# More of an MLP's up projection by seven products of halves, and its down product made in one piece of five parts

## The chip, the cores and the metric

One Trainium2 chip, one of its cores. The metric is the device time of one execution in microseconds (us); lower is better. Kernel before: median 923.41 us of 3 runs (923.1 to 926.32).

## What is computed

A decoder trunk of one layer on 512 tokens of width 1024, all in float32: three token mixers with an output projection, then a gated MLP with a causal depthwise convolution, then a last norm. The change lies in the MLP:

```python
h2 = rms_norm(x, norm_ffn[l])                                        # 512 x 1024
up = causal_dwconv(h2 @ w_up[l], ffn_conv_w[l], ffn_conv_b[l])       # 512 x 6144
gate_h, val_h = jnp.split(up, 2, axis=-1)
x = x + (jax.nn.gelu(gate_h, approximate=True) * val_h) @ w_down[l]  # w_down 3072 x 1024
...
return rms_norm(x, final_norm)
```

## The kernel before

**Products.** Each float32 operand is split into a high and a low fp32r part (`split`, L95: ScalarE (ACT) writes the high part, L97, VectorE (DVE) the rest, L98), and each product is three TensorE (PE) matmuls, high by high, high by low and low by high (`mm3`, L100 to L104).

**Units.** The program is a list of units of PE work. Each has preparations, (lead, function) pairs, and `emit` (L183) writes a preparation out that many units ahead of its unit. The engines' queues keep very nearly the order in which this is written; each engine works through its queue in order.

**Up projection.** The 6144 channels are 24 pairs of a gate tile and a value tile of 128 channels. A *plain* pair is two units (`up_units`, L1187), each 24 matmuls of 512 columns and one 512 KB weight load, split two units ahead (`AHEAD`). A *fast* pair (`up_fast`, L1240) is made by seven products of halves (Winograd's form of Strassen's scheme): the pair's weights are four blocks B11 to B22 of 128 x 512, the tokens and the inner dimension are halved, and there are seven units a1, a2, c1, c2, b1, b2, b3, each 12 matmuls of 256 columns. Block sums are made by DMA: `load` (SP's queue) brings one block, and `add` (L1255, POOL's queue) adds another to it in SBUF. So B11 is split for a1, gets B12 added, is split for c1, gets B22 added, is split for b1, gets B21 added, is split for b3. DVE and ACT put the seven results together from PSUM (L1273 to L1278). Then `up_evac` (L1167: one ACT and two DVE instructions per tile, the convolution) and `up_mix` (L1182: gelu on ACT, product on DVE at L1184) give the activations of that tile.

In time, fast pairs overlap: one beat of eight units is b1 of the pair before, a1, a plain unit, b2 of the pair before, c1, a2, b3 of the pair before, c2.

**Down product.** Activations of tiles 0 to 19 (five *parts* of four tiles) are multiplied with `w_down` by seven products as well (`seven`, L285, with `down_fast`, L1297). Here a key (a1, a2, c1, c2, b1, b2, b3) has one unit per part, 12 matmuls of 512 columns in two PSUM banks, and after the last part the banks are read into the residual `x2` (`read`, L1337: one DVE instruction of 512 columns per bank and target, L1335). The preparations of an a1 unit are `sums` (L1301: six DVE instructions of 256 columns on the activations of its four tiles, three units ahead) and `act_ready` (L1324, the split of the sums, one unit ahead); of all, the weights' split two units ahead. Before, this is two calls, of three parts and of two; the second adds its a1 banks to what the first kept (`kept`, L1343). `blend` (L353) mixes plain units in: the 21 units of the first call among 14 plain ones (tiles 13 to 19), the 14 of the second among 8 (tiles 20 to 23, whose product goes by `halves`, L1402, to a last plain down product).

**Memory.** Tiles of 128 x 512 live in 51 slots (`NSLOT`); split weights of 1024 columns in four buffers for the high and four for the low parts (`NWB`, tags `whi`, `wlo`), so that the split of a weight waits for the end of the unit that used the buffer four weights earlier; whole 512 KB loads in three (`NRAW`).

Of the kernel before, what the change touches and what calls it, by code (L numbers as in the profile page):

```python
# [34 lines left out]
NF = FF // P  # L35
# [22 lines left out]
def trunk(ctx: ExitStack, tc: tile.TileContext, x, xT, mem, memT, par, wdecay, wch, wv, wg, wmk,  # L58
# [285 lines left out]
    def run(*parts):  # L344

        for p in parts:
            if isinstance(p, tuple):
                unit(*p)
            else:
                for v in p:  # L350
                    made_unit(*v) if isinstance(v, tuple) else step(v)

    def blend(us, fast, steps=()):  # L353

        for i, u in enumerate(us):
            unit(*u)
            for l, f in ((fast, lambda v: made_unit(*v)), (steps, step)):
                for v in l[len(l) * i // len(us):len(l) * (i + 1) // len(us)]:
                    f(v)
# [407 lines left out]
    b2 = [u for d in range(KD) for u in branch(2, oc, d)]  # L767
# [472 lines left out]
    def up_fast(i, keep):  # L1240

        src = lambda q: wup[NF * (int(q[2]) - 1) + i][:, HB * (int(q[1]) - 1):HB * int(q[1])]
        raw, w, st = {}, {}, {}

        def load(q):
            raw[q] = fslot()
            loads.append(nc.sync.dma_start(raw[q], src(q)))

        def ready(key, q, more=None):
            w[key] = rslot(), rslot()  # L1250
            split(*w[key], raw[q])
            if more:
                add(q, more)

        def add(q, more):  # L1255
            nc.gpsimd.dma_start(raw[q], src(more), accum_op=ALU.add)

        def run(key):
            if key == "a1":
                st["x"], st["o"] = bank((P, HT)), (fslot(), fslot())  # L1260
            elif key in ("a2", "c1"):
                st[key] = sbank((P, HT))
            ps = st["c1" if key[0] == "c" else "a2" if key == "a2" else "x"]
            hi, lo = w.pop(key)
            k = range(KD // 2)
            mm3(ps, [(*(a[:, j * P:(j + 1) * P] for a in (hi, lo)), *h2_part(key, j)) for j in k],
                key in ("a1", "a2", "c1"), True, key not in ("a1", "a2", "c1"))
            (g, v), tt = st["o"], nc.vector.tensor_tensor

            one, two = slice(0, HT), slice(HT, S)  # L1270
            if key in ("a1", "c1", "c2", "b3"):
                o = {"a1": g[:, one], "c1": v[:, two], "c2": v[:, one], "b3": g[:, two]}[key]
                nc.scalar.activation(o, ps, AF.Copy)  # L1273
            elif key == "a2":
                tt(out=g[:, one], in0=g[:, one], in1=ps, op=ALU.add)
            else:
                o = v[:, one if key == "b1" else two]
                tt(out=o, in0=o, in1=ps, op=ALU.subtract)  # L1278
            if key == "b3":
                up_mix(*(up_evac(a, NF * half + i) for half, a in enumerate((g, v))), i, keep)  # L1280

        pre = {
            "a1": [(8, lambda: load("B11")), (3, lambda: ready("a1", "B11", "B12"))],
            "a2": [(6, lambda: load("B21")), (3, lambda: ready("a2", "B21"))],
            "c1": [(2, lambda: ready("c1", "B11", "B22"))],
            "c2": [(6, lambda: load("B22")), (3, lambda: ready("c2", "B22"))],
            "b1": [(2, lambda: ready("b1", "B11", "B21"))],
            "b2": [(9, lambda: load("B12")), (6, lambda: add("B12", "B22")), (3, lambda: ready("b2", "B12"))],
            "b3": [(2, lambda: ready("b3", "B11"))],
        }  # L1290
        return {key: (p, lambda key=key: run(key)) for key, p in pre.items()}
# [105 lines left out]
    acts = {}  # L1397
# [4 lines left out]
    def halves(i, a):  # L1402
        acts[i] = rslot(), rslot()
        split(*acts[i], a)

    group = lambda first: lambda k: acts[first + k]
    us = up_units((0, 1, 2, 5, 8, 11), whole, 3)
    run(*us[:3], [lambda: h2_sums(0)], us[3], [lambda: h2_sums(1)], us[4], [lambda: h2_ready("c1", 0), lambda: h2_ready("c1", 1)],
        us[5], [lambda: h2_ready("c2", 0), lambda: h2_ready("c2", 1)])

    ahead = None
    for i, u in zip((3, 4, 6, 7, 9, 10), us[6:]):
        f = up_fast(i, whole)
        run([ahead["b1"]] if ahead else [], [f["a1"]], u)
        run([ahead["b2"]] if ahead else [], [f["c1"], f["a2"]], [ahead["b3"]] if ahead else [], [f["c2"]])
        if not ahead:
            run([lambda k=k, p=p: h2_ready(k, p) for k in ("b1", "b2") for p in range(2)])
        ahead = f
    us = up_units(range(12, 20), whole)
    run([ahead["b1"]], us[0], [ahead["b2"]], us[1], [ahead["b3"]])  # L1420
    blend(us[2:], down_fast(0, 3, group(0), True, False))
    blend(up_units(range(20, NF), halves), down_fast(3, 2, group(12), False, True))
    step(lambda: gain_rows(gfin))
    weave(down_units(wdown2, group(20), final, None, final_left, 2), [])

    emit()

# [90 lines left out]
```

## Time and profile before

| | |
|---|---|
| median of 3 runs | 923.41 us |
| profiled execution: time, span | 924.37 us, 922.6 us |
| PE busy | 912.0 us (99% of the span), 4606 matmuls |
| DVE busy | 657.2 us (71%) |
| ACT busy | 524.1 us (57%) |
| POOL busy | 128.1 us (14%) |
| granted PE clock, mean | 0.997 |

A row of the time line gives the start, the length, engine, line, operation and tiles, with `xN` for N merged instructions and in brackets the idle time before it and what ended it. Instructions of one engine overlap a little at their ends, so the step from start to start is what one costs in a queue without gaps, not its length. About 540 us into the span the up projection begins; the first down call stands at about 684 to 815 us, the second at 815 to 896 us.

### The profile page before, as it was taken

How to read it: one execution, taken by the hardware profiler on the slowest of the kernel's cores; microseconds unless marked ns; L12 is line 12 of the kernel's file. 1: busy time of each engine (PE TensorE's matmuls, PEld its weight loads, DVE VectorE, ACT ScalarE, POOL GpSimd, SP SyncE). 2: the span in 40 equal slices, each digit the busy share in tenths (PEclk: the TensorE clock that was granted, in tenths of full speed). 3: DMA queues.
4: the chain of work that ended last, by engine and by line, in shares of the span. 5: the costliest groups of instructions: out<-in, count | busy, mean ns of one | idle time of the engine just before them, and what ended most of it. 6: DMA issues, size and time to landing. Idle time of an engine off the chain costs nothing.

```text
span 922.6 us, 12732 instructions
## 1 busy us (share of the span) xinstructions
PE 912.0 (99%) x4606; PEld 784.1 (85%) x4606; DVE 657.2 (71%) x1168; ACT 524.1 (57%) x888; POOL 128.1 (14%) x168
## 2 busy tenths in 40 slices
PE   9999999999999999999999999999999999999997
PEld 7899888888889998888888898998988888888885
DVE  6997755665689568746766678767787757598765
ACT  7765655685865468474534446555555445445544
POOL 0010000000243430320000000222111130013102
PEclk9999999999999999999999999999999999999998
DMA  7446223213467884321157313675646785357622
GB/s 238 148 137 214 92 88 101 88 42 119 110 170 167 187 204 126 115 86 53 52 157 258 116 59 90 157 185 130 148 114 165 145 228 125 114 137 181 139 69 91
DMA packets 51183, 123.27 MB, mean 134 GB/s; under 512 B 6145, under 2 KB 14001, under 8 KB 51121
## 3 DMA queue, kind: packets, MB, share of 16 engines
q1 hardware_dynamic: 35648, 94.99, 31.6%
q0 software_dynamic: 15328, 27.21, 17.3%
q8 instruction: 36, 0.59, 0.3%
q10 hardware_dynamic: 144, 0.26, 0.1%
q14 instruction: 27, 0.21, 0.1%
HBM read 117.99 MB, written 3.67 MB: 132 GB/s over the span
## 4 chain that ended last, share of the span: by engine, by line
PE 87%; DMA 5%; DVE 3%; issue 2%; ACT 2%; POOL 0%; SPq 0%; DVEq 0%; POOLq 0%; ACTq 0%
PE mm L104 78%; DMA f<-in_wup 4%; PE sm L104 3%; DMA f<-in_wv 2%; PE mm L436 2%; DVE wlo L98 1%; DVE r L98 1%; ACT r L97 1%; PE sm L211 0%; PE sm L996 0%; PE sm L983 0%; PE sm L1010 0%; DVE f L810 0%; PE sm L1147 0%; PE sm L601 0%
## 5 line engine op out<-in xcount | busy, mean ns | idle before, releaser
L97 ACT ACTIVATE whi<-raw 128x1024 fp32r<-128x1024 f32 (+3 forms) x142 | 135.5, 961 | 144.4 <-PE mm L104 113.1
L98 DVE TENSOR_TENSOR wlo<-raw,whi 128x1024 fp32r<-128x1024 f32 (+3 forms) x142 | 157.4, 1113 | 82.8 <-ACT whi L97 39.4
L104 PE MATMUL mm<-whi,r 128*128 128x512 f32 (+2 forms) x568 | 171.2, 372 | 0.0
L104 PEld LDWEIGHTS mm<-whi,r 128*128 128x128 f32 x568 | 105.5, 188 | 15.9 <-ACT r L97 0.3
L104 PE MATMUL mm<-hh,whi 128*128 128x512 f32 x288 | 113.4, 394 | 0.0
L104 PE MATMUL mm<-hl,whi 128*128 128x512 f32 x288 | 112.8, 392 | 0.0
L104 PE MATMUL mm<-wlo,r 128*128 128x512 f32 (+2 forms) x284 | 105.7, 372 | 0.5 <-DVE wlo L98 0.5
L104 PE MATMUL mm<-h2l,whi 128*128 128x512 f32 x264 | 102.8, 390 | 0.0
L104 PE MATMUL mm<-h2h,whi 128*128 128x512 f32 x264 | 102.7, 390 | 0.0
L98 DVE TENSOR_TENSOR r<-f,r 128x512 fp32r<-128x512 f32 (+3 forms) x144 | 79.7, 577 | 23.0 <-ACT r L97 22.7
L104 PE MATMUL mm<-r,whi 128*128 128x512 f32 (+1 forms) x432 | 94.2, 367 | 0.0
L97 ACT ACTIVATE r<-f 128x512 fp32r<-128x512 f32 (+3 forms) x144 | 70.1, 535 | 34.1 <-DMA f<-in_wup 29.2
L98 DVE TENSOR_TENSOR wlo<-f,whi 128x512 fp32r<-128x512 f32 (+2 forms) x90 | 53.8, 631 | 47.5 <-ACT whi L97 40.6
L104 PEld LDWEIGHTS mm<-r,whi 128*128 128x128 f32 x432 | 75.2, 189 | 13.1
L97 ACT ACTIVATE whi<-f 128x512 fp32r<-128x512 f32 (+2 forms) x90 | 48.2, 579 | 62.5 <-PE mm L104 48.8
L104 PE MATMUL mm<-hh,wlo 128*128 128x512 f32 x288 | 71.4, 390 | 0.0
L104 PE MATMUL mm<-r,r 128*128 128x512 f32 (+2 forms) x336 | 65.7, 346 | 0.3 <-ACT r L97 0.3
L104 PE MATMUL mm<-h2h,wlo 128*128 128x512 f32 x264 | 65.2, 389 | 0.0
L104 PEld LDWEIGHTS mm<-hh,wlo 128*128 128x128 f32 x288 | 54.0, 188 | 11.2
L104 PEld LDWEIGHTS mm<-hh,whi 128*128 128x128 f32 x288 | 54.1, 188 | 10.8
L104 PEld LDWEIGHTS mm<-hl,whi 128*128 128x128 f32 x288 | 54.1, 188 | 10.7
L104 PEld LDWEIGHTS mm<-r,r 128*128 128x128 f32 (+1 forms) x336 | 53.3, 186 | 9.6 <-ACT r L97 0.5
(261 smaller groups left out, 1545.2 us busy)
## 6 DMA issues: line engine op xcount, KB each, us to landing
raw<-in_wch SPq DMA_DIRECT2D x39, 512.0 KB, 3.3
raw<-in_wup SPq DMA_DIRECT2D x36, 512.0 KB, 4.0
f<-in_wdown POOLq DMA_DIRECT2D x40, 256.0 KB, 7.0
raw<-in_wbr SPq DMA_DIRECT2D x24, 384.0 KB, 3.1
raw<-in_wdown SPq DMA_DIRECT2D x14, 512.0 KB, 3.8
f<-in_wup SPq DMA_DIRECT2D x24, 256.0 KB, 6.9
f<-in_wup POOLq DMA_DIRECT2D x24, 256.0 KB, 6.4
f<-in_wdown SPq DMA_DIRECT2D x20, 256.0 KB, 4.7
```

What stands on the lines that cost most here:

```text
L97: nc.scalar.activation(hi, src, AF.Copy)
L98: return (eng or nc.vector).tensor_tensor(out=lo, in0=src, in1=hi.bitcast(F32), op=ALU.subtract)
L104: nc.tensor.matmul(ps, lhsT=l, rhs=r, start=first and i == 0, stop=last and i == len(seq) - 1, skip_group_check=more)
L436: nc.tensor.matmul(ps[u], lhsT=w(a, u, k), rhs=xs["r"][k][j], start=k == 0 and i < n, stop=k == KD - 1 and i >= len(seq) - n)
```

## The change

Tiles 12, 13, 15, 16 and 18 become fast pairs too (eleven in place of six), each in a beat with a plain unit of tiles 5, 8, 11, 14, 17, 19. The down product is one call of five parts, its 35 units blended with the seven plain units that are left (the second of tile 20, then tiles 21, 22, 23): one plain unit, then five units of one key. Some leads change.

```diff
         pre = {
-            "a1": [(8, lambda: load("B11")), (3, lambda: ready("a1", "B11", "B12"))],
-            "a2": [(6, lambda: load("B21")), (3, lambda: ready("a2", "B21"))],
-            "c1": [(2, lambda: ready("c1", "B11", "B22"))],
+            "a1": [(10, lambda: load("B11")), (5, lambda: ready("a1", "B11", "B12"))],
+            "a2": [(7, lambda: load("B21")), (3, lambda: ready("a2", "B21"))],
+            "c1": [(3, lambda: ready("c1", "B11", "B22"))],
             "c2": [(6, lambda: load("B22")), (3, lambda: ready("c2", "B22"))],
             "b1": [(2, lambda: ready("b1", "B11", "B21"))],
-            "b2": [(9, lambda: load("B12")), (6, lambda: add("B12", "B22")), (3, lambda: ready("b2", "B12"))],
+            "b2": [(10, lambda: load("B12")), (7, lambda: add("B12", "B22")), (1, lambda: ready("b2", "B12"))],
             "b3": [(2, lambda: ready("b3", "B11"))],
         }
...
-    group = lambda first: lambda k: acts[first + k]
-    us = up_units((0, 1, 2, 5, 8, 11), whole, 3)
+    us = up_units((0, 1, 2), whole, 3)
...
+    us = up_units((5, 8, 11, 14, 17, 19), whole) + up_units(range(20, NF), halves)
     ahead = None
-    for i, u in zip((3, 4, 6, 7, 9, 10), us[6:]):
+    for i in (3, 4, 6, 7, 9, 10, 12, 13, 15, 16, 18):
         f = up_fast(i, whole)
-        run([ahead["b1"]] if ahead else [], [f["a1"]], u)
+        run([ahead["b1"]] if ahead else [], [f["a1"]], us.pop(0))
...
-    us = up_units(range(12, 20), whole)
-    run([ahead["b1"]], us[0], [ahead["b2"]], us[1], [ahead["b3"]])
-    blend(us[2:], down_fast(0, 3, group(0), True, False))
-    blend(up_units(range(20, NF), halves), down_fast(3, 2, group(12), False, True))
+    run([ahead["b1"]], us.pop(0), [ahead["b2"]], us.pop(0), [ahead["b3"]])
+    blend(us, down_fast(0, 5, lambda k: acts[k], True, True))
     step(lambda: gain_rows(gfin))
-    weave(down_units(wdown2, group(20), final, None, final_left, 2), [])
+    weave(down_units(wdown2, lambda k: acts[20 + k], final, None, final_left, 2), [])
```

How the queues stand at the start of the down product, at three places. *a1_0, a1_1, ...* are the a1 units of parts 0, 1, ...

**First place: DVE, where the weights of the first a1 units are split.** Before, the rows that begin with the split of a1_1's weights (`wlo_1312`). `f_1297` is the value half of plain tile 12, `f_1300` and `f_1301` the halves of fast tile 10, `f_1284` the gate half of tile 12.

```order
L98 TENSOR_TENSOR wlo_1312_6716<-f_1287_6571,whi_1311_6715 128x512
L98 TENSOR_TENSOR wlo_1312_6716<-f_1288_6572,whi_1311_6715 128x512
L1171 SCALAR_TENSOR_TENSOR f_1297_6631<-mm_1296_6606,prm_76,f_1297_6631 128x511
L1171 SCALAR_TENSOR_TENSOR f_1297_6631<-mm_1296_6606,prm_76,f_1297_6631 128x510
L1171 SCALAR_TENSOR_TENSOR f_1300_6656<-f_1255_6359,prm_76,f_1300_6656 128x511
L1184 TENSOR_TENSOR f_1284_6563<-f_1284_6563,f_1297_6631 128x512
L1171 SCALAR_TENSOR_TENSOR f_1300_6656<-f_1255_6359,prm_76,f_1300_6656 128x510
```

Of the change, the rows that begin with the split of a1_2's weights (`wlo_1471`). `f_1449` is the gate half of plain tile 20, `f_1456` and `f_1457` are the halves of fast tile 18; L1311 to L1313 are `sums`.

```order
L98 TENSOR_TENSOR wlo_1471_7653<-f_1439_7486,whi_1470_7652 128x512
L1311 TENSOR_TENSOR f_1452_7556<-f_1185_5944,f_1113_5533 128x256
L1171 SCALAR_TENSOR_TENSOR f_1449_7546<-mm_1448_7521,prm_76,f_1449_7546 128x511
L1312 TENSOR_TENSOR f_1453_7557<-f_1452_7556,f_1185_5944 128x256
L1171 SCALAR_TENSOR_TENSOR f_1449_7546<-mm_1448_7521,prm_76,f_1449_7546 128x510
L1313 TENSOR_TENSOR f_1185_5944<-f_1185_5944 128x256
L1311 TENSOR_TENSOR f_1452_7556<-f_1215_6127,f_1245_6308 128x256
L1171 SCALAR_TENSOR_TENSOR f_1456_7581<-f_1405_7271,prm_76,f_1456_7581 128x511
```

At both places the first row waits for its buffer, so for the end of the plain unit just ahead of the last pair's b3. Of the change it is followed at once by the sums of part 1, with the evacuations of tiles 18 and 20 between them.

**Second place: DVE, up to the split of a1_1's activation sums.** Before, `r_1318` (the low part of a1_1's sums) stands 24 rows behind `wlo_1312`, and the sums that precede it are those of parts 1 and 2.

```order
L1171 SCALAR_TENSOR_TENSOR f_1310_6711<-mm_1309_6686,prm_76,f_1310_6711 128x510
L1312 TENSOR_TENSOR f_1314_6722<-f_1313_6721,f_1173_5865 128x256
L1313 TENSOR_TENSOR f_1173_5865<-f_1173_5865 128x256
L1311 TENSOR_TENSOR f_1313_6721<-f_1300_6656,f_1233_6229 128x256
L98 TENSOR_TENSOR r_1318_6744<-f_1184_5942,r_1317_6743 128x256
```

Of the change, `f_1465` is the value half of plain tile 20, `r_1467` the low part of tile 20's activations (needed by the last down product only), `r_1469` the low part of a1_1's sums, 30 rows behind `wlo_1471`.

```order
L1171 SCALAR_TENSOR_TENSOR f_1465_7636<-mm_1464_7611,prm_76,f_1465_7636 128x511
L98 TENSOR_TENSOR wlo_1471_7653<-f_1440_7487,whi_1470_7652 128x512
L1171 SCALAR_TENSOR_TENSOR f_1465_7636<-mm_1464_7611,prm_76,f_1465_7636 128x510
L98 TENSOR_TENSOR wlo_1479_7687<-f_1446_7517,whi_1478_7686 128x512
L1184 TENSOR_TENSOR f_1449_7546<-f_1449_7546,f_1465_7636 128x512
L98 TENSOR_TENSOR wlo_1479_7687<-f_1447_7518,whi_1478_7686 128x512
L98 TENSOR_TENSOR wlo_1485_7719<-f_1454_7564,whi_1484_7718 128x512
L98 TENSOR_TENSOR r_1467_7643<-f_1449_7546,r_1466_7642 128x512
L98 TENSOR_TENSOR r_1469_7647<-f_1185_5944,r_1468_7646 128x256
```

The product of tile 20 (L1184), its split, and the weights of a1_2, a1_3 and a1_4 now stand ahead of a1_1's sums.

**Third place: ACT, the high part of a1_1's sums.** Before (`r_1317`), behind tile 13's gate half and a plain unit's weights:

```order
L1169 ACTIVATE f_1310_6711<-mm_1309_6686,prm_76 128x512
L97 ACTIVATE whi_1326_6794<-raw_1325_6792 128x1024
L97 ACTIVATE r_1317_6743<-f_1184_5942 128x256
L97 ACTIVATE r_1317_6743<-f_1214_6125 128x256
L1183 ACTIVATE f_1310_6711<-f_1310_6711 128x512
```

Of the change (`r_1468`), behind the weights of a1_4 (`whi_1484`, whose buffer is free when a1_0 ends) and the high part of tile 20's activations (`r_1466`, which waits for DVE's L1184 of `f_1449`):

```order
L1169 ACTIVATE f_1465_7636<-mm_1464_7611,prm_76 128x512
L97 ACTIVATE whi_1484_7718<-f_1454_7564 128x512
L97 ACTIVATE whi_1484_7718<-f_1455_7565 128x512
L97 ACTIVATE r_1466_7642<-f_1449_7546 128x512
L97 ACTIVATE r_1468_7646<-f_1185_5944 128x256
L97 ACTIVATE r_1468_7646<-f_1215_6127 128x256
```

PE's a1_1 unit begins with `r_1468`. On PE, before, a plain unit stands between a1_0 and a1_1; of the change a1_1 follows a1_0 at once.

## Rows read from the trace of the kernel before

**Rows 1.** The profile page: span, and the busy time of PE and DVE.
```profile
span 922.6 us, 12732 instructions
PE 912.0 (99%) x4606; PEld 784.1 (85%) x4606; DVE 657.2 (71%) x1168; ACT 524.1 (57%) x888; POOL 128.1 (14%) x168
```

**Rows 2.** Who waited for whom, PE's rows over the whole span: total us, times, longest. The two longest.
```profile
PE sm L211 <- DVE warm L207: 1.1, 1, 1.1
PE mm L104 <- DVE f L1278: 0.7, 1, 0.7
```

**Rows 3.** Time line of PE in a beat of fast pairs: one unit of a fast pair (601.02 to 602.46), then one plain unit (602.46 to 607.93).
```profile
601.02 0.28 PE L104 MATMUL mm<-h2h,r 128*128 128x256 f32 x1
...
602.46 0.40 PE L104 MATMUL mm<-h2h,whi 128*128 128x512 f32 x1
...
606.11 1.98 PE L104 MATMUL mm<-h2h,wlo 128*128 128x512 f32 x8
607.93 1.60 PE L104 MATMUL mm<-r,r 128*128 128x256 f32 x12
```

**Rows 4.** Time line of PE at the start of the down product: a1_0 (684.17 to 686.89), a plain unit, and two more down units (692.33 to 697.80).
```profile
684.17 0.39 PE L104 MATMUL mm<-whi,r 128*128 128x512 f32 x1
...
686.89 0.39 PE L104 MATMUL mm<-h2h,whi 128*128 128x512 f32 x1
...
692.33 0.39 PE L104 MATMUL mm<-whi,r 128*128 128x512 f32 x1
...
697.80 0.39 PE L104 MATMUL mm<-h2h,whi 128*128 128x512 f32 x1
```

**Rows 5.** Busy time by stage: stretch, its length, then us busy (and instructions) of PE, weight loads, DVE, ACT, POOL, the granted clock, the share of the DMA engines, GB/s. Three beats of fast pairs; the first down call; the second.
```profile
602.00:649.00 47.00, 46.28 (x315) 42.63 (x314) 32.58 (x53) 26.21 (x48) 9.07 (x11) 1.00 0.67 158
682.00:815.00 133.00, 133.00 (x589) 110.04 (x588) 95.43 (x161) 67.14 (x110) 19.35 (x22) 1.00 0.57 140
815.00:896.00 81.00, 81.00 (x358) 66.92 (x357) 66.46 (x110) 42.06 (x70) 12.32 (x14) 1.00 0.56 144
```

**Rows 6.** Time line of DVE at the start of the first down call.
```profile
677.53 1.29 DVE L98 TENSOR_TENSOR wlo<-f,whi 128x512 fp32r<-128x512 f32 x2 [0.80 <-PE mm L104]
...
680.85 0.69 DVE L1184 TENSOR_TENSOR f<-f,f 128x512 f32<-128x512 f32 x1
681.45 1.41 DVE L1171 SCALAR_TENSOR_TENSOR f<-f,prm,f 128x510 f32<-128x510 f32 x2
...
684.71 0.76 DVE L1311 TENSOR_TENSOR f<-f,f 128x256 f32<-128x256 f32 x2
685.38 0.42 DVE L1312 TENSOR_TENSOR f<-f,f 128x256 f32<-128x256 f32 x1
...
687.71 0.74 DVE L1171 SCALAR_TENSOR_TENSOR f<-mm,prm,f 128x510 f32<-128x510 f32 x1
688.37 0.42 DVE L1312 TENSOR_TENSOR f<-f,f 128x256 f32<-128x256 f32 x1
...
691.92 2.35 DVE L98 TENSOR_TENSOR wlo<-raw,whi 128x1024 fp32r<-128x1024 f32 x2
694.19 0.74 DVE L1171 SCALAR_TENSOR_TENSOR f<-mm,prm,f 128x511 f32<-128x511 f32 x1
```

**Rows 7.** Time line of ACT at the same place.
```profile
676.67 1.25 ACT L97 ACTIVATE whi<-f 128x512 fp32r<-128x512 f32 x2 [2.16 <-DMA f<-in_wdown]
677.83 0.76 ACT L1169 ACTIVATE f<-mm,prm 128x512 f32<-128x512 f32 x1
...
688.06 0.70 ACT L97 ACTIVATE r<-f 128x256 fp32r<-128x256 f32 x2
688.67 0.62 ACT L1183 ACTIVATE f<-f 128x512 f32<-128x512 f32 x1
```

**Rows 8.** The chain that ended last, in order of time, around PE's one wait of the up projection: start, us, what.
```profile
615.43 8.77 DMA f<-in_wup
624.20 0.02 issue
...
628.24 0.34 DVE f L1278
628.58 0.14 issue
628.72 1.91 PE mm L104 x12
```

**Rows 9.** Busy time by half microseconds at the end of the span, columns as in rows 5. PE's last matmul ends at 915.66 us.
```profile
915.50:916.00 0.50, 0.16 (x1) 0.00 (x0) 0.30 (x1) 0.50 (x1) 0.00 (x0) 1.00 0.82 307
...
917.00:917.50 0.50, 0.00 (x0) 0.00 (x0) 0.26 (x2) 0.44 (x3) 0.00 (x0) 1.00 0.85 319
917.50:918.00 0.50, 0.00 (x0) 0.00 (x0) 0.43 (x3) 0.00 (x0) 0.00 (x0) 0.83 0.69 246
918.00:918.50 0.50, 0.00 (x0) 0.00 (x0) 0.46 (x2) 0.29 (x1) 0.00 (x0) 0.50 1.03 389
```

**Rows 10.** DMA issues: queue, count, KB each, median us from issue to landing.
```profile
f<-in_wdown POOLq DMA_DIRECT2D x40, 256.0 KB, 7.0
f<-in_wup SPq DMA_DIRECT2D x24, 256.0 KB, 6.9
f<-in_wup POOLq DMA_DIRECT2D x24, 256.0 KB, 6.4
f<-in_wdown SPq DMA_DIRECT2D x20, 256.0 KB, 4.7
```

## The prediction

> **What bounds the kernel now.** I read the profile page first. PE is busy for 912.0 of 922.6 us, DVE for 657.2 [rows 1]. Then the waits: the longest that PE spends on another engine are 1.1 us at the very start and 0.7 us once in the up projection [rows 2]. So PE's queue is the time: whatever leaves it shortens the run, unless a gap opens. The third view, busy time by stage, shows where a gap could open. In the beats of fast pairs DVE works 32.6 of 47 us and ACT 26.2; in the first down call DVE works 95.4 of 133; in the second, with fewer plain units beside the down units, 66.5 of 81, which is 82% [rows 5]. PE waits in neither down call, but DVE is the engine that is nearest to it.
>
> All sums are made against the profiled execution, 924.37 us, which is 0.96 us above the median of the runs; I carry the difference over to the median, 923.4. A change below 0.5% (4.6 us, so 918.8 to 928.0) cannot be told from none.
>
> **The change part by part.**
>
> *PE's work.* A unit of a fast pair takes 602.46 - 601.02 = 1.44 us and a plain unit 607.93 - 602.46 = 5.47 us, from start to start [rows 3]. A plain pair is 2 x 5.47 = 10.94 us, a fast one 7 x 1.44 = 10.08: 0.86 us less. Five pairs change: **-4.3 us**. The saving is small because seven products of half the columns cost almost what two full units do. The down product keeps its 35 units of 2.73 us (two of them take 697.80 - 692.33 = 5.47 us [rows 4]): 0.
>
> *Five more beats.* A beat lasts 7 x 1.44 + 5.47 = 15.5 us and loads the other engines as the present ones do (DVE 69%, ACT 56%, DMA 158 GB/s [rows 5]). All work that comes with it (seven splits, eight 256 KB transfers in place of two of 512 KB per pair, the combining on DVE) is hidden there now, so 0. Without that cover one late accumulation per beat would cost what the one wait costs today, 0.7 us [rows 2].
>
> *The leads.* That one wait hangs on an accumulation that took 8.77 us to land [rows 8]: ACT and DVE stood behind it, and a subtraction that PE needed came late. The new leads give the split of B11 for a1 two units more and that for c1 one, so each accumulation on that chain starts earlier against its use. Between 0 and -0.7; I take **-0.4**, rather more than half, since the other beats with the old leads already run without a wait. The split for b2 moves from three units ahead to one, but that one is the plain unit of 5.47 us and the split is 0.6 on ACT and 0.6 on DVE: 0. The loads that go ahead on SP's queue by one or two units hold slots longer; up to eighteen tiles of activations are held by then, but each load still has three or more units to land in (6.9 us [rows 10] against four units, at least 5.8 us, and a lead of three more before PE needs it): 0.
>
> *Reads of the down product.* One call of five parts reads the banks once: 14 DVE instructions of 512 columns go, 14 x 0.6 = 8.4 us of DVE. They end after PE has moved on, so this is worth nothing on the path: 0.
>
> *The start of the down product.* Here the price lies. Before, a plain unit stands between a1_0 and a1_1 (684.17 to 686.89, then to 692.33 [rows 4]); of the change five a1 units follow each other, with all `sums` in front. First what DVE has to do, by steps from start to start: 0.60 us for 512 columns (680.85 to 681.45), 0.66 for the convolution (687.71 to 688.37), 0.335 for 256 columns (two of them, 684.71 to 685.38) [rows 6]. Call T the end of the plain unit ahead of the last b3; the split of a1_2's weights waits for it, as its like does at 677.53 today [rows 6], and all of DVE's queue behind it too.
> - DVE from there to the product of tile 20 (L1184), 27 instructions: 5 x 0.60 + 8 x 0.66 + 14 x 0.335 = 13.0 us.
> - ACT then writes the high part of tile 20's activations, 0.6 (two of 512 take 677.83 - 676.67 = 1.16), and the first half of a1_1's sums, 0.4 (two of 256 take 688.67 - 688.06 = 0.61, and the end of one overlaps the next) [rows 7]. With 0.2 for the handoffs a1_1 can start at T + 14.2.
> - PE from T: b3 1.44, a plain unit 5.47, a1_0 2.73: T + 9.6.
>
> PE waits 4.6 us. The low part of the sums comes after three more DVE instructions of 512 and one of 256 columns, T + 13.0 + 2.1 and a handoff, where PE wants it four matmuls (0.9 us) into a1_1, at T + 15.1: 0.2 more. **+4.8**. It can be no less than ACT alone makes it: the weights of a1_4 wait for the end of a1_0 and stand ahead of that split, so 1.16 + 0.6 + 0.4 = 2.1. It can be 7.0 if DVE's instructions cost their full lengths (0.69, 0.75, 0.42 [rows 6] make 15.3). I take the steps, because that stretch of DVE's queue is without gaps today.
>
> DVE stays behind through a2, where the six subtractions and additions of a1's banks and the ten sums for c2 fall, but by my count never by more than those 4.8 us, and from c1 on it has some 14 us of work (5 x 3 x 0.60 for the splits, 5 for reads and the plain unit) in 19 of PE. So there is one gap, and no second.
>
> *The clock.* At the end of the span PE's last matmul ends at 915.66 us; the granted clock still reads 1.00 up to 917.50 and then falls, 0.83 in the next half microsecond and 0.50, that is 1.2 GHz, from 918.0 on [rows 9]. So some 2.2 us without matmuls were enough there. A gap of 4.6 us is twice as long, and no other gap of the trace is; I expect the fall, and PE comes back at half speed. The price is bounded by 0 (the clock holds, or is back at once) and by the four a1 units behind the gap at half speed, 4 x 2.73 = 10.9 us. No row shows how fast it returns. I take **+1.4**, half a unit's work lost, near the lower end, since DVE is late there anyway and part of the slow time would have been waiting.
>
> The Trainium skill, "TensorE: Matmul & The Clock Gate", section "What's actually happening", has throttled as the default state, released by activity, so that an engine that has stood idle starts slow. By that rule the gap costs more than its own length; the trace agrees at the end of the span (0.50) and shows no return. With a clock that holds, the sum is that of rival A.
>
> *Sum.* -4.3 - 0.4 + 4.8 + 1.4 = +1.5: 925.9 against the profiled execution, **925.0** against the median. The saving of PE's work is spent on one wait for DVE and ACT.
>
> **The rivals.**
> - *A, the clock holds.* The same gap, no fall: 923.4 - 4.7 + 4.8 = 923.5. For it: the granted clock is 0.997 over the whole run. Against it: the fall within 2.2 us in rows 9.
> - *B, ACT alone makes the gap.* If DVE gets through its queue faster than I count, 2.1 us are left, hardly enough for the clock: 920.8. Against it: the steps repeat within 0.02 us.
> - *C, the whole gain.* If the order is absorbed (the gap is hidden by work that I place too late): 918.7, faster. Against it: ACT's 2.1 us follow from the order alone.
> - *D, the last blocks of the down product come late (slower).* The B12 loads of five parts wait for slots, the last until b1_1 ends. Till b2_4 PE has three b1 units, a plain one and four b2 units, 8.2 + 5.5 + 10.9 = 24.6 us; the load takes 4.7, the accumulation 7.0 [rows 10], the splits and POOL's issue some 2.8: 14.5. It decides when the two transfers take 21.8 us, not 11.7. At twice their time b2_4 is 1.6 us late, at three times 13.3; the middle is 7.5, so 932.5. For it: both calls' transfers now come in 133 us in place of 215. Against it: 10 us of slack, and the second call does the same beside 144 GB/s without a wait [rows 5].
> - *E, the clock stays low* for all four units: 923.4 - 4.7 + 4.8 + 10.9 = 934.4 at most, or with part of it some 930.
>
> **How the numbers follow.** My forecast 0.57, A 0.20, B 0.05, C 0.05, D 0.08, E 0.05. Faster is C and the lowest edge of B: 0.06. Slower is D, E and the upper edge of the forecast (gap 7.0 and more than one unit's clock, 923.4 - 4.7 + 7.0 + 2.7 = 928.4): 0.16. Same: 0.78. The likeliest time is 925.0. The range takes in A, B and the forecast with its bounds: from 919.5, halfway from B to C, to 929.0, that upper edge and 0.6 us of the runs' own spread; it leaves out D, E and most of C.
>
> **What would show it.** In the changed profile: PE's waits should list one of 4 to 5 us for ACT L97 or DVE L98, at the second down unit, a1_1, with a granted clock below 1 in the few microseconds behind it; the beats should still be 15.5 us long with waits below 0.5 us; DVE should be busy without a gap from T to the end of a2. I am wrong if PE shows no wait above 2 us there, if the beats of tiles 12 to 18 are longer than the first ones, or if PE waits for an accumulation of `w_down` in b2 or b3.

## The result, and the profile after

The change takes 927.14 us (median of 20 runs, 925.12 to 928.26) against 925.54 for the kernel before, run beside it as often: ratio 1.0021, 95% interval [1.0013, 1.0029], so 1.2 to 2.7 us slower. That lies within the 0.5% that the prediction called no change. It had forecast +1.5 us; seen: +1.9 by the ratio, 1.6 between the medians. The forecast time, 925.0, lies 2.1 us below the measured one because it was counted from 923.41, the median of three runs of the kernel before.

The page, and who PE waited for (total us, times, longest), answering to [rows 1] and [rows 2]:

```profile
span 925.1 us, 13276 instructions
PE 909.3 (98%) x4786; PEld 789.6 (85%) x4786; DVE 664.7 (72%) x1194; ACT 538.1 (58%) x933; POOL 145.3 (16%) x188
```
```profile
PE mm L104 <- ACT r L97: 4.6, 1, 4.6
PE sm L211 <- DVE warm L207: 1.1, 1, 1.1
PE sm L1147 <- DVE f L1129: 0.7, 1, 0.7
```

PE has less to do and one long wait. Where it stands, by the time lines of PE (answering to [rows 4]), DVE [rows 6] and ACT [rows 7]; the bracket is the idle time ahead and what ended it:

```profile
761.60 0.39 PE L104 MATMUL mm<-whi,r 128*128 128x512 f32 x1
...
763.87 0.61 PE L104 MATMUL mm<-whi,r 128*128 128x512 f32 x2
769.05 0.50 PE L104 MATMUL mm<-whi,r 128*128 128x512 f32 x1 [4.57 <-ACT r L97]
```
```profile
754.96 0.69 DVE L98 TENSOR_TENSOR wlo<-f,whi 128x512 fp32r<-128x512 f32 x1 [0.74 <-ACT whi L97]
755.57 0.42 DVE L1311 TENSOR_TENSOR f<-f,f 128x256 f32<-128x256 f32 x1
...
767.35 0.68 DVE L1184 TENSOR_TENSOR f<-f,f 128x512 f32<-128x512 f32 x1
767.95 1.28 DVE L98 TENSOR_TENSOR wlo<-f,whi 128x512 fp32r<-128x512 f32 x2
```
```profile
764.52 1.15 ACT L97 ACTIVATE whi<-f 128x512 fp32r<-128x512 f32 x2 [1.94 <-PE mm L104]
768.06 2.47 ACT L97 ACTIVATE r<-f 128x512 fp32r<-128x512 f32 x7 [2.39 <-DVE f L1184]
```

Read across: a1_0 runs from 761.60. DVE starts on its backlog at 754.96 and comes to the product of tile 20 (L1184) at 767.35. ACT is idle for 2.39 us for that product, with a1_1's sums behind it in its queue; a1_1 starts at 769.05. DVE is without a gap from 754.96 to 802.9, past the end of the a2 units, as the prediction asked for.

The clock behind it, stage by stage (columns as in [rows 5]; the clock stands after POOL):

```profile
768.00:769.00 1.00, 0.00 (x0) 0.00 (x0) 1.00 (x3) 0.94 (x3) 0.82 (x1) 1.00 0.49 45
769.00:770.00 1.00, 0.95 (x3) 0.81 (x4) 1.00 (x3) 1.00 (x4) 0.84 (x2) 0.79 1.02 180
770.00:771.00 1.00, 1.00 (x4) 0.64 (x3) 1.00 (x4) 0.53 (x2) 0.91 (x2) 0.50 0.60 92
...
773.00:774.00 1.00, 1.00 (x6) 0.80 (x5) 1.00 (x4) 0.31 (x1) 0.00 (x0) 1.00 1.12 195
```

The full beats (those with a pair before them), by the starts of their plain units: 15.54 us each, from the second to the tenth, eight intervals in 124.32 us [rows 3]. The first line starts the first plain unit of the up projection, the last one the final 48 matmuls:

```profile
548.88 0.63 PE L104 MATMUL mm<-h2h,whi 128*128 128x512 f32 x2
...
603.44 0.40 PE L104 MATMUL mm<-h2h,whi 128*128 128x512 f32 x1
...
727.76 0.40 PE L104 MATMUL mm<-h2h,whi 128*128 128x512 f32 x1
...
906.81 11.04 PE L104 MATMUL mm<-r,r 128*128 128x512 f32 x48
```

**A yardstick for what follows.** I measure the *stage*, from the first plain unit (548.88 here) to those 48 matmuls: 357.93 us, before 904.62 - 547.55 = 357.07. It leaves out what lies ahead of the changed code, whose length differs by several us between executions, as will be seen. *Excess* is what the beats take over 15.54 us each, counted from the second full beat on. Of the kernel before, whose second full beat has its plain unit at 602.46 [rows 3] and the fifth and last at 650.81, it is 48.35 - 3 x 15.54 = 1.73:

```profile
547.55 0.63 PE L104 MATMUL mm<-h2h,whi 128*128 128x512 f32 x2
...
650.81 0.40 PE L104 MATMUL mm<-h2h,whi 128*128 128x512 f32 x1
...
904.62 11.04 PE L104 MATMUL mm<-r,r 128*128 128x512 f32 x48
```

### The profile page after: what moved, and what is told of

Same layout as the page of the kernel before. It is cut to its first block, busy times and chain, and to the rows that moved or that the text cites. A ratio compares the mean times of both kernels' runs of the same rounds, so it can differ in the third digit from the quotient of the medians.

```text
span 925.1 us, 13276 instructions
## 1 busy us (share of the span) xinstructions
PE 909.3 (98%) x4786; PEld 789.6 (85%) x4786; DVE 664.7 (72%) x1194; ACT 538.1 (58%) x933; POOL 145.3 (16%) x188
## 4 chain that ended last, share of the span: by engine, by line
PE 88%; DVE 5%; DMA 3%; ACT 2%; issue 1%; SPq 0%; POOL 0%; DVEq 0%; ACTq 0%; POOLq 0%
PE mm L104 76%; PE sm L104 7%; DMA f<-in_wv 2%; PE mm L436 2%; DVE wlo L98 1%; DVE f L1171 1%; DVE r L98 1%; ACT whi L97 1%; DMA raw<-in_wup 0%; ACT r L97 0%; PE sm L996 0%; PE sm L983 0%; PE sm L1010 0%; DMA raw<-in_wch 0%; DVE f L810 0%
## 5 line engine op out<-in xcount | busy, mean ns | idle before, releaser
L98 DVE TENSOR_TENSOR wlo<-raw,whi 128x1024 fp32r<-128x1024 f32 (+3 forms) x132 | 145.1, 1105 | 80.5 <-ACT whi L97 43.7
L97 ACT ACTIVATE whi<-raw 128x1024 fp32r<-128x1024 f32 (+3 forms) x132 | 125.0, 953 | 117.7 <-PE mm L104 89.0
L97 ACT ACTIVATE r<-f 128x512 fp32r<-128x512 f32 (+3 forms) x179 | 91.0, 551 | 41.4 <-DMA f<-in_wup 34.4
L98 DVE TENSOR_TENSOR r<-f,r 128x512 fp32r<-128x512 f32 (+3 forms) x179 | 100.8, 598 | 6.6 <-ACT r L97 6.2
L1256 POOL DMA_DIRECT2D f<-in_wup x44 | 38.5, 989 | 285.4 <-PE sm L1147 131.2
L104 PE MATMUL mm<-r,r 128*128 128x256 f32 (+2 forms) x456 | 81.9, 329 | 0.0
L104 PEld LDWEIGHTS mm<-r,r 128*128 128x128 f32 (+1 forms) x456 | 68.7, 187 | 10.3 <-ACT r L97 0.7
L104 PE MATMUL mm<-h2l,whi 128*128 128x512 f32 x184 | 71.8, 390 | 0.0
L104 PE MATMUL mm<-h2h,whi 128*128 128x512 f32 x184 | 71.6, 390 | 0.0
```

Of the source, the lines that this page charges most:

```text
L97: nc.scalar.activation(hi, src, AF.Copy)
L98: return (eng or nc.vector).tensor_tensor(out=lo, in0=src, in1=hi.bitcast(F32), op=ALU.subtract)
L104: nc.tensor.matmul(ps, lhsT=l, rhs=r, start=first and i == 0, stop=last and i == len(seq) - 1, skip_group_check=more)
```

## The experiments

All ratios go against runs of the kernel before that were taken together with those of the version. Traces come from one execution per kernel; durations in the table are read off their time lines. *1.73 of 3* is the excess in three intervals. The longest wait is PE's, at a down unit or a plain unit beside it.

| kernel | median us | ratio to before, 95% | first plain unit | stage | excess | longest wait |
|---|---|---|---|---|---|---|
| before | 924.59 to 925.54 | 1 | 547.55 | 357.07 | 1.73 of 3 | none |
| the change | 927.14 | 1.0021 [1.0013, 1.0029] | 548.88 | 357.93 | 0 of 8 | 4.57 |
| again | 927.61 | 1.0026 [1.0012, 1.0041] | 549.76 | 362.08 | 3.34 of 8 | 4.56 |
| fill | 925.89 | 1.0014 [1.0000, 1.0028] | 547.15 | 356.34 | 0 of 8 | (filled) |
| latesplit | 924.02 | 0.9987 [0.9975, 0.9999] | 547.96 | 354.79 | 0.25 of 8 | 1.15 |
| latesplit2 | 922.60 | 0.9977 [0.9965, 0.9989] | 549.15 | 354.58 | 0.48 of 8 | 1.15 |
| best | 927.36 | 1.0027 [1.0015, 1.0039] | 550.05 | 357.29 | 0.03 of 8 | 1.99 |
| alllate | 927.36 | 1.0022 [1.0004, 1.0039] | 547.10 | 357.27 | 0 of 8 | 2.57 |
| spread | 931.87 | 1.0075 [1.0055, 1.0094] | 547.31 | 361.44 | 0 of 8 | 5.36 |
| twocalls | 931.02 | 1.0070 [1.0055, 1.0085] | 547.39 | 362.69 | 0 of 8 | 5.10 |
| onedown | 926.97 | 1.0032 [1.0018, 1.0046] | 547.60 | 359.11 | 0.46 of 3 | 1.21 |
| beflead | 925.52 | 1.0011 [0.9997, 1.0024] | 548.84 | 356.89 | 0 of 3 | 0.49 |
| lead8 | 927.70 | 1.0036 [1.0022, 1.0051] | 550.87 | 358.46 | 0.14 of 8 | 4.57 |
| oldlead | 928.14 | 1.0042 [1.0029, 1.0055] | 548.79 | 359.43 | 1.88 of 8 | 4.57 |

### Where the 4.57 us come from: latesplit, and once more as latesplit2

```diff
     def halves(i, a):
+        if i == 20:
+            late20.append(a)
+            return
...
+    fast = down_fast(0, 5, lambda k: acts[k], True, True)
+    pre, fn = fast[5]
+    fast[5] = pre, lambda: (fn(), split20())
+    blend(us, fast)
```

> The changed kernel with one step moved: the split of tile 20's activations (high part on ACT, low part on DVE), which only the last down product needs, is written behind a2_0 instead of ahead of the sums of a1_1. Theory (the 4.57 us wait is ACT standing in its queue behind the split of tile 20, which waits for DVE's product of that tile): ACT makes the high part of a1_1's sums as soon as a1_0 has freed its weight buffers; the wait before a1_1 shrinks to 0.5 to 2 us, the clock holds, and the time is 3 to 5 us below that of the change, if no new wait of its size opens. Rival (DVE is that late with the sums themselves and the low parts, whatever stands on ACT): the wait before a1_1 stays at 2.5 us or more, or comes back as long at one of the next units, and the time is within 1.5 us of the change.

> The kernel of the run latesplit (tile 20's split behind a2_0, nothing else) once more, unaltered. Theory (its gain is in the order, not in the execution): PE waits 1.1 to 1.2 us for ACT's whi at the plain unit of tile 21 and nowhere 4 us, clock 1.00 until the last matmul; the stretch from the first plain unit to the last 48 matmuls is 354.8 us plus whatever the beats lose to accumulations; the time is 1 to 2 us below before. Rival (the first run was a lucky chip): same as before or slower by more than 0.5 us.

The wait before a1_1 is gone. PE now waits 1.15 us, some two units on, for a plain unit's weights:

```profile
760.51 0.39 PE L104 MATMUL mm<-whi,r 128*128 128x512 f32 x1
...
767.74 0.50 PE L104 MATMUL mm<-h2h,whi 128*128 128x512 f32 x1 [1.15 <-ACT whi L97]
```
```profile
761.39 0.72 ACT L97 ACTIVATE r<-f 128x256 fp32r<-128x256 f32 x2
763.43 1.16 ACT L97 ACTIVATE whi<-f 128x512 fp32r<-128x512 f32 x2 [1.32 <-PE mm L104]
766.63 1.06 ACT L97 ACTIVATE whi<-raw 128x1024 fp32r<-128x1024 f32 x1 [2.04 <-PE mm L104]
```

ACT makes the sums of a1_1 at 761.39, before a1_0 ends, not 4 us after it. The stage is 3.1 us shorter, the run about 1.2 us (second time 2.1) below before. This is the fastest version, both times. So the wait was a price of order: the same work is done without it.

One step was moved, but the queues changed at more places: they keep the written order less closely than the description of the kernel says. On ACT the sums of a1_1 now also stand ahead of a1_4's weights (763.43). On PE three matmuls of the plain unit (767.74) stand between a1_1 and a1_2. On DVE the low parts of a1_1's sums (764.39 is the first) stand ahead of tile 20's product; in the change they stand behind it, as the last two of the three in this row. Of the change, then of latesplit:

```profile
769.15 1.35 DVE L98 TENSOR_TENSOR r<-f,r 128x512 fp32r<-128x512 f32 x3
```
```profile
764.39 0.42 DVE L98 TENSOR_TENSOR r<-f,r 128x256 fp32r<-128x256 f32 x1
...
765.71 0.69 DVE L1184 TENSOR_TENSOR f<-f,f 128x512 f32<-128x512 f32 x1
```

PE wants these low parts four matmuls (0.9 us) into a1_1, so by these rows DVE's order alone would have held it for some 4 us. That the order made the wait is shown; that ACT's one step alone made it is not.

The 1.15 us left are ACT's split of 1.06, for which it waited 2.04 us until a1_1 had ended: a wait for a buffer, not for DVE. The gain is less than wait and clock together (6.3 us): these 1.15 us come in, and down units further on lose some tenths here and there (the longest 0.24, at 788.62, for DVE's low parts).

### The clock: fill

```diff
+    def fill():
+        ps = sbank()
+        for i in range(20):
+            nc.tensor.matmul(ps, lhsT=h2["h"][:, 0, 0:P], rhs=h2["h"][:, 1, :], start=i == 0, stop=i == 19)
```

> The changed kernel with 20 matmuls of 512 columns more, written right behind a1_0 into a spare PSUM bank and read by nobody, so that PE is busy through the wait for the sums of a1_1. They take 20 x 0.227 = 4.5 us, about the length of the wait (4.57). Theory (the granted clock falls because PE stands still, and the clock then costs 1.7 us on the path): the clock stays 1.00 behind a1_0, a1_1 takes 2.73 us instead of 4.44, and the time is 1.5 to 1.8 us below that of the change. Rival 1 (the slow time hides in a wait that would be there anyway, because DVE is late through a2): a1_1 is shorter, but PE waits about as much more later, and the time is within 0.4 us of the change. Rival 2 (the clock falls for another reason than PE standing still): half clock stays behind the wait, same time.

```profile
759.39 0.39 PE L104 MATMUL mm<-whi,r 128*128 128x512 f32 x1
...
762.11 4.69 PE L1424 MATMUL sm<-h2h 128*128 128x512 f32 x20
766.85 0.50 PE L104 MATMUL mm<-whi,r 128*128 128x512 f32 x1
...
778.30 0.39 PE L104 MATMUL mm<-h2h,whi 128*128 128x512 f32 x1
```
```profile
769.00:773.00 4.00, 4.00 (x19) 3.26 (x18) 4.00 (x13) 2.29 (x5) 0.00 (x0) 1.00 0.98 160
```

The clock holds. From a1_0 to the next plain unit it is 778.30 - 759.39 = 18.91 us, of the change 781.67 - 761.60 = 20.07: 1.16 us less. DVE is busy throughout (4.00 of 4 us), and small waits take the rest of the 1.72 that half clock costs (a1_1: 773.49 - 769.05 = 4.44 in place of 2.72). So theory, with a part of rival 1, from one trace of each kernel. By the ratios the run is 0.6 us below the change, give or take 1.5 (the halves of both intervals, put together as a root of squares): from the run times alone it is not shown.

### Is it the one call, or the missing plain units? onedown, twocalls, spread

onedown (the kernel before) and twocalls (the change):

```diff
-    blend(us[2:], down_fast(0, 3, group(0), True, False))
-    blend(up_units(range(20, NF), halves), down_fast(3, 2, group(12), False, True))
+    run(*us[2:])
+    blend(up_units(range(20, NF), halves), down_fast(0, 5, group(0), True, True))
```
```diff
-    blend(us, down_fast(0, 5, lambda k: acts[k], True, True))
+    blend(us[:4], down_fast(0, 3, lambda k: acts[k], True, False))
+    blend(us[4:], down_fast(3, 2, lambda k: acts[12 + k], False, True))
```

spread:

```diff
-    blend(us, down_fast(0, 5, lambda k: acts[k], True, True))
+    fast = down_fast(0, 5, lambda k: acts[k], True, True)
+    for k, n in enumerate((1, 1, 1, 1, 1, 15, 15)):
+        unit(*us[k])
+        for _ in range(n):
+            made_unit(*fast.pop(0))
```

> The kernel before (six fast pairs, old leads) with the down product alone changed: the eight plain units of tiles 13 to 16 and those of 17 to 19 run ahead of it, then one call of five parts, its 35 units blended with the eight plain units of tiles 20 to 23. PE's work is that of before. Theory (the 4.6 us are not a price of one call as such; they come from where the change puts tile 20's split and the evacuations of tiles 18 and 20 in DVE's and ACT's queues): no wait above 2 us, two of 1 to 1.5 us for ACT's whi, no fall of the clock, the stretch from the first plain unit to the last 48 matmuls 357.1 + 1.5 to 3, and the time 1 to 3 us above before. Rival (one call of five parts packs the sums of a1 so that PE waits for them wherever it stands): a wait of 3 us or more at a1_1 with a fall of the clock, 4 us or more above before.

> The changed kernel with the down product back in two calls of three and two parts (21 units blended with four of the seven plain units, then 14 with three); eleven fast pairs and the new leads stay. Theory (the wait before a1_1 comes from taking the plain units away for fast pairs, so that a1 units follow each other, and not from one call): the wait of 4 to 5.5 us and the half clock behind it stay; reading the banks twice adds about 1 to 3 us of waits where the second call starts; the time is 0 to 4 us above the change. Rival (one call is what costs; two calls with eleven pairs would keep the saving of 4.2 us of PE's work): no wait above 2 us, and 2 us or more below before.

> The changed kernel with the seven plain units placed elsewhere among the 35 units of the down product: one of its units behind each of the first five, 15 behind each of the last two; nothing else moves. Each a1 unit then has a plain unit ahead of it, as before. Theory (the wait before a1_1 is DVE's lag, 4.6 us, less than a plain unit of 5.47): that wait is gone or below 1 us and the clock holds there; but the two runs of 15 down units without a plain unit leave DVE and ACT behind, and a wait of 3 to 6 us opens in them, so the time is within 2 us of the change. Rival (DVE has slack there): no wait above 1.5 us anywhere and 4 to 6 us below the change.

PE's waits, of onedown, of twocalls, and two lines of ACT in spread:

```profile
PE mm L104 <- ACT whi L97: 2.4, 2, 1.2
```
```profile
PE mm L104 <- ACT r L97: 5.3, 2, 5.1
PE mm L104 <- ACT whi L97: 2.3, 2, 1.2
```
```profile
854.68 0.78 ACT L1169 ACTIVATE f<-mm,prm 128x512 f32<-128x512 f32 x1 [2.08 <-PE mm L104]
...
858.80 1.15 ACT L97 ACTIVATE r<-f 128x512 fp32r<-128x512 f32 x2 [2.30 <-DVE f L1184]
```

One call with its plain units run ahead has no long wait: theory. It is not free there: the stage grows by 2.0 us, by 3.3 if the beats' excess is left out (1.73 and 0.46), and the run by 3.0, [1.7, 4.3]; how much of that is the one call and how much the thinner cover of plain units is not separated. Two calls keep the long wait, and the second call adds two of 1.2 us. So one call by itself does not make the long wait, and with eleven fast pairs two calls are 4.5 us worse still, at or a little past the upper end of what I expected. In spread the wait at a1_1 is gone as expected (0.26 left), and one of 5.36 us stands in the run of 15 units without a plain unit, ACT again behind a split (now of tile 23) that waits for its L1184. Its price is 5 us over the change, not 2: a miss of size (stage +3.5), which one trace does not explain. Nor is it DVE's lag, as I expected: the evacuation of that tile (L1169, 854.68) had itself waited 2.08 us until a unit of PE ended, and DVE stood idle for it for 2.01 us.

### Can it be had without any wait? best and alllate

best is latesplit with 1, 1, 3, 6, 8, 8 and 8 down units behind the seven plain units, by the loop shown for spread. alllate:

```diff
+    for i, j in zip(range(20, NF), (6, 12, 23, 33)):
+        pre, fn = fast[j]
+        fast[j] = pre, lambda fn=fn, i=i: (fn(), split_late(i))
+    for k, n in enumerate((1, 2, 4, 6, 7, 7, 8)):
```

> The changed kernel with the split of tile 20 written behind a2_0 (as in the run latesplit) and the seven plain units placed by hand among the 35 units of the down product: 1, 1, 3, 6, 8, 8 and 8 units of it behind them, so that plain units stand beside a1 and a2, where DVE and ACT are late, and few later, in place of 5 behind each. Theory (PE waits at the start of the down product because DVE's and ACT's work for a1 and a2 is packed beside too little of PE's): the wait of 1.15 us that latesplit kept is gone, one of 0.6 us may come late, the stretch from the first plain unit to the last 48 matmuls is 353.2 to 354.2 us (353.0 would be the sum without any wait), against 354.79 of latesplit and 357.93 of the change, and the time about 4 us below the change, 2 below before. Rival (the stretch with few plain units makes DVE late there): a wait of 1.5 us or more in c1 to b3, 355 us or more.

> The changed kernel with the splits of all of tiles 20 to 23 (not of tile 20 alone) written some down units after their products, behind the 7th, 13th, 24th and 34th unit of the down product, and 1, 2, 4, 6, 7, 7 and 8 of its units behind the seven plain ones. Theory (each wait of PE at a down unit of best, latesplit and the change is ACT standing behind the split of such a tile, which waits for DVE's product of it): no wait above 0.5 us at a down unit, the clock stays 1.00 to the last matmul, the stretch from the first plain unit to the last 48 matmuls is 353.0 to 353.7 us, and the time is 3 us below before, about 5 below the change. Rival (DVE's work for a1, a2 and the reads is late by itself): a wait of 1 us or more stays, 354.5 us or more.

Both fail, and the rivals hold. PE's waits in best, then in alllate:

```profile
PE mm L104 <- ACT r L97: 2.0, 1, 2.0
```
```profile
PE mm L104 <- DVE m L1335: 2.6, 1, 2.6
```

The start of the down product has no wait above 0.5 us in either. At 876 us, two or three down units behind the last plain one, a wait of 2.0 or 2.6 us opens: in best for a sum behind tile 23's split, in alllate, with that split out of the way, for DVE's reads of the banks (L1335). So there PE waits for DVE's own queue; whether another order of that queue would bring the reads forward is not tested. In neither placing did seven plain units cover both ends. Both waits cost clock too:

```profile
877.00:878.00 1.00, 0.00 (x0) 0.00 (x0) 1.00 (x3) 0.95 (x3) 0.00 (x0) 1.00 0.00 0
878.00:879.00 1.00, 0.96 (x4) 0.67 (x4) 1.00 (x3) 1.00 (x4) 0.00 (x0) 1.00 0.00 0
879.00:880.00 1.00, 1.00 (x4) 0.55 (x4) 1.00 (x4) 1.00 (x4) 0.00 (x0) 0.87 0.00 0
880.00:881.00 1.00, 1.00 (x4) 0.81 (x3) 1.00 (x3) 1.00 (x4) 0.00 (x0) 0.50 0.00 0
```

(best.) PE is back at 878.04 and the clock falls to 0.50 some 1.7 us later.

### The leads, and the later start: beflead, lead8, oldlead, again

beflead is the kernel before with the change's table of leads, oldlead the change with the table of before (both tables stand in the diff of the change). lead8:

```diff
-            "a1": [(10, lambda: load("B11")), (5, lambda: ready("a1", "B11", "B12"))],
+            "a1": [(8, lambda: load("B11")), (5, lambda: ready("a1", "B11", "B12"))],
```

> The kernel before with the changed leads alone (B11 two units earlier on SP's queue and its split for a1 two earlier, the others as in the change); six fast pairs and two down calls stay. Theory after the two traces (the beats of before held 1.73 us over 4 x 15.54, all of which the leads take away, and the earlier load of B11 makes the transposes ahead of the up projection wait about 0.7 us): all beats 15.54 us from start to start, a wait of about 0.7 us at L1147, and the time about 1 us below before. Rival 1 (the leads are worth only the one listed wait, 0.4 to 0.7 us): within 0.5 us of before. Rival 2 (the excess of 1.73 us in the beats of before belonged to that one execution): beats of before and of this kernel alike.

> The changed kernel with a single number put back: the load of B11 for a1 stands 8 units ahead in place of 10. Theory (with 10, one B11 load stands ahead of the first plain units' loads on SP's queue, which come about 1 us later for it; norm and transposes in front of the up projection then wait 0.66 us): that wait is gone, the start of the first plain unit is 1.0 to 1.3 us earlier from the start of the span, the rest is the same, and the time is 0.7 to 1.3 us below that of the change. Rival (the later start is chance of one execution): first plain unit at 548.9 us as in the change, same time within 0.4 us. If the beats need the load that early, waits of up to 0.5 us each come back in the beats.

> The changed kernel with the leads of before: eleven fast pairs and one down call stay. Theory (an accumulation takes 5.3 to 8.8 us to land from one execution to the next, and the new leads let PE wait for fewer of them): the ten beats hold 1 to 4 us of excess over 10 x 15.54, the wait of 4.57 us before a1_1 stays within 0.2 us, and the time is 0.5 to 3 us above the change. Rival (the excess is chance alone, the leads are worth nothing): excess below 0.3 us here, and the time within 0.5 us of the change.

> The changed kernel once more, unaltered, in the call of the run alllate. Theory (the wait of 4.57 us is fixed by the order; where the up projection starts and how long half clock lasts is chance of one execution): the wait before a1_1 is 4.5 to 4.65 us again; the first plain unit starts anywhere between 547 and 551 us; the stretch from there to the last 48 matmuls is 357.9 us, or up to 1 us more where half clock lasts longer. Rival (the later start belongs to the change): the first plain unit at 548.8 us or later with a wait of about 0.7 us at L1147.

*The later start.* My theory, that a B11 load now stands ahead of the first plain units' loads, falls. lead8 puts the old order back there and has the longest wait at L1147 (1.5 us) and the latest start (550.87), and its run is 1.4 us above the change by the ratios, give or take 1.5, where I expected 0.7 to 1.3 below. Five kernels whose code up to there is that of the change (fill, latesplit, alllate, spread, twocalls) start between 547.10 and 547.96; again, latesplit2 and best, with that same code, at 549.15 to 550.05. oldlead, with the leads of before, waits 0.8 us too. The rival in again asked for a late start with that wait, and its execution shows both, but those five decide: it is chance of one execution, worth up to 3 us. The stage of again, 362.08, is outside what I expected (357.9, or up to 1 us more): its beats hold 3.34 us of excess, and its half clock lasts 6.8 us.

*The leads.* With the new ones the beats were clean to 0.5 us in ten of eleven traces, in again not:

```profile
651.08 0.40 PE L104 MATMUL mm<-h2h,whi 128*128 128x512 f32 x1
...
657.80 1.88 PE L104 MATMUL mm<-r,r 128*128 128x256 f32 x12 [1.09 <-ACT r L97]
...
668.15 0.40 PE L104 MATMUL mm<-h2h,whi 128*128 128x512 f32 x1
```

and its chain ahead of that wait (start, us, what), the same link as in [rows 8]:

```profile
648.46 7.32 DMA f<-in_wup
655.78 0.02 issue
655.81 0.02 ACT r L97
```

The accumulations' median landing in the change, in again and in oldlead, as POOL's queue issues them [rows 10]:

```profile
f<-in_wup POOLq DMA_DIRECT2D x44, 256.0 KB, 5.4
```
```profile
f<-in_wup POOLq DMA_DIRECT2D x44, 256.0 KB, 6.4
```
```profile
f<-in_wup POOLq DMA_DIRECT2D x44, 256.0 KB, 6.7
```

The three traces with old leads held 1.73, 0.46 and 1.88 us of excess. oldlead is slower than the change by 1.0042 - 1.0021 = 0.0021, with the two intervals' halves put together as a root of squares 0.0015: 2.0 ± 1.4 us. So there the new leads look worth something, though lead8, with one load put back, came out 1.4 us above the change too; in the kernel before (beflead) they gain nothing: +1.0 us, [-0.3, +2.2]. There the start of the down product is 0.94 us longer in the one trace (650.00 to 687.02 in place of 650.81 to 686.89), with two waits for DVE's low parts: half of what the beats gain. My theory of beflead (1 us faster) misses.

## Why the prediction was right, point by point

- **PE's work, -4.3.** Right. From before to the change the stage grows by 0.86 us. Wait (4.57), clock (1.72) and a last beat's fragment that is 0.48 us longer add 6.77; the excess of before (1.73) goes; so the rest is 0.86 - 6.77 + 1.73 = -4.2. It is a remainder, and 0.35 of it lies ahead of the second full beat (54.56 us from the start of the stage in place of 54.91).
- **Start of the down product, +4.8.** Right in place, cause and size: the 27 DVE instructions up to L1184 took 767.95 - 754.96 = 13.0 us as counted, the wait 4.57, against 4.6 and a second one of 0.2 that the trace does not list. Five executions with this order gave 4.56 or 4.57 (the change, again, lead8, oldlead) and 5.10 (twocalls, with other weights ahead). That ACT alone would still leave 2.1 us (the lower bound, and rival B) is not shown: in latesplit a1_4's weights, on which that bound rests, no longer stand ahead of the sums, and no wait is left at a1_1.
- **The clock, +1.4.** Right, 1.2 on the path (fill) of 1.72 lost. Rival A, in which it holds, did not happen. My remark in B that 2.1 us were hardly enough for the clock was wrong: best lost it after 2.0.
- **Reads, 0.** Right for the change. In alllate the same reads make PE wait 2.6 us: the cover is the plain units ahead of them.
- **The leads, -0.4, and five more beats, 0.** Here the sizing fails. I took one listed wait (0.7) of one execution for the stock of what leads can give. The beats of that execution were 1.73 us long over their work, mostly in waits too small to be listed, and how much they hold changes with the execution: in the change 0 us the first time and 3.34 the second, with accumulations landing in 5.4 and 6.4 us. The measured worth is 2.0 ± 1.4 in the changed kernel, nothing in the one before. That the sum came out so near (+1.5 against +1.9) is partly luck: all its terms lie in the stage, which grew by 0.86 us in the one pair of traces, as the beats gave 1.73 where I had put 0.4. Where the rest of the 1.9 us lies is not shown.
- **SP's earlier loads, 0.** Nothing shown against it. **D**: no wait for a `w_down` accumulation in b2 or b3 of the change: did not happen. **E**: half clock lasted 3.4 us there, not four units.

What stays open is whether the change also costs something ahead of the stage: single traces vary there by 3 us, and the intervals of the medians are no narrower than 1.5 us.

## What to carry to other kernels

When two engines feed a third, look in the feeders' queues for work that isn't due yet and stands ahead of work that is, above all if it waits for another feeder: writing one such split later, with the shifts in the queues that came of it, turned +1.9 us into -1.2 to -2.1. Look at the queues behind such a move too: more may have shifted than was written. Units that only keep TensorE busy are cover; count how many are left before converting them into cheaper work, since the saving (here 4.2 us) is spent where the cover ends. And read a listed wait of one execution as a sample: compare the lengths of repeated pieces, and more than one execution, before pricing it.

## What the runs showed of the hardware

- The granted clock fell to 0.50 (1.2 GHz) after waits of PE of 1.99 (best), 2.57 (alllate), 4.56 or 4.57 (the change, again, lead8, oldlead), 5.10 (twocalls) and 5.36 us (spread), and in no trace after waits of 1.13 to 1.59 (the longest of these at 106.39 in lead8). It can fall when PE is already back, 3.7 us behind the last matmul in best and 5.1 in the change, or while it still waits, 3 us behind it in lead8 (769.0, a1_1 from 770.60). It was back after 3.4 us in the change and after 6.8 in lead8, with the same wait ahead: 1.7 and 2.6 us lost.
- The Trainium skill, "TensorE: Matmul & The Clock Gate", section "What's actually happening", lets an engine that stood idle start slow. The 0.50 behind these waits agrees with it, but a1_1 of the change started at 1.00 and became slow 0.5 us later.
- An accumulation of 256 KB into SBUF took 5.1 to 6.7 us in the median from trace to trace of nearly the same program, and the longest one of a trace 7.7 (fill) to 9.1 (oldlead). In two executions of one program, the change and again, it was 5.4 and 6.4 us, and the beats held 0 and 3.34 us of excess; that the landings make the excess is argued from the one chain above, not shown.
